# S5 heads of a two-layer hybrid backbone: rotation tables doubled on VectorE, swapped halves made by matmuls and multiplied out of PSUM

## The chip, the cores and the metric

One core of one Trainium2 chip. The metric is the device time of one execution in microseconds (us). TensorE is PE, VectorE DVE, ScalarE ACT, GpSimd POOL, SyncE SP; SP issues the DMAs spoken of here.

## The reference

Two layers over 128 context and 512 latent tokens, d_model 1024, fp32. Layer 0 has S5 heads and neighbourhood attention behind one input projection, layer 1 a gated DeltaNet; each has an MLP. The change lies in the S5 heads of layer 0:

```python
def _s5_scan(u, lam_re, lam_im, log_dt, b_re, b_im, c_re, c_im, x0):
    lam = lax.complex(lam_re, lam_im)
    lam_bar = jnp.exp(lam * jnp.exp(log_dt)[:, None])
    b_bar = ((lam_bar - 1) / lam)[..., None] * lax.complex(b_re, b_im)
    bu = jnp.einsum('gnp,blgp->blgn', b_bar, u)
    bu = bu.at[:, 0].add(lam_bar * x0)
    # x_t = lam_bar * x_(t-1) + bu_t
    _, xs = lax.associative_scan(comb, (a, bu), axis=1)
    y = jnp.einsum('gpn,blgn->blgp', c_mat, xs).real
    return y, xs[:, -1]
```

There are 32 groups of 16 channels with 64 complex states each, run forward and backward; the outputs of both directions and d * u are added, then gelu and a sigmoid gate. The context's last states are an output.

## The kernel before, in words

The tokens are cut into chunks of 8, 64 of latents and 16 of context, with one place more for each run's starting state: 82 columns, in segments of 65 and 17. The recurrence goes over chunks. The heads are worked in four **batches** of 8 groups (`s5_batch`), each with two **units**, one for each direction d (`s5_unit`). The real parts of the states lie on rows 0 to 63, the imaginary ones on rows 64 to 127.

A unit builds input weights `bp` on DVE (L783, L784; the sum L785 on POOL for d = 0), transposes them on PE (L790) and copies them out with ACT (L791). It builds output weights `ct` on DVE (L796 to L798), and multiplies the inputs `U` by the input weights on PE (L807). ACT copies the result to `W` (L809). The recurrence has a complex factor. The kernel turns the frame by e^(i theta e), so that the scan has a real factor: a rotation before (`rotate(W, SU, Z)`), the scan (L842, L844), a rotation back (`rotate(Y, AD, Sv)`). A rotation needs the other half of the rows: `swap` moves halves by two DMAs (L823, L824), DVE multiplies by the cosine (L830) and the sine (L831), in two segments of 65 and 17 chunks, and L832 adds, on POOL for d = 0.

`s5_tables` makes the cosine and sine tables of a batch: three doublings by `turns` on POOL (L861 to L866) from the first eight powers `s5e`, which `s5_params` makes with the same helper; then three DMAs of `rt` (L878, L879) bring both directions on all rows. `s5_taps` makes the taps of the convolution inside a chunk: small matmuls (L912), two ACT copies, DVE (L917, L919), then through DRAM into `L`. `s5_back` makes a batch's outputs with three matmuls to a group (L945, L947, L949) and its gelu (L962 to L967).

`even_s5` writes the four batches first, at a high priority, and then `project()` at a low one: the projection of queries, keys and values, 12 blocks of weights, each in two halves of 320 columns of 24 matmuls (L205 to L207; weights split in two parts, L194 on ACT and L196). ACT copies a half from the PSUM tile `pg` to `qs` (L1093, in the pool's buffers `us`); keys and values are transposed (L1096, L1108) into the PSUM tile `pc`. A scheduler sorts the whole into one order on each engine by readiness and priority. Buffers of a tag are handed out in the order of the program text, and an operation can't stand ahead of one that still holds its buffer. PSUM has four tags, `pa`, `pb`, `pc` and `pg`, with two buffers each; `us` has two, `rt` two, `bp`, `bpt` and the scratch `s5tmp` one. `proj_u`, the projection of the S5 inputs, runs before all of that; attention (L1001) after it.

```python
    def ps(self, tag):
        return self.psum.tile([128, 512], F32, name=tag, tag=tag, bufs=2)
...
            with tc.high_priority(offset=4000):
                cur = self.s5_batch(b, P, Us[b]) if b < 4 else None
...
        with tc.high_priority(offset=-500):
            project()
```

Of the kernel before, what the change touches and what calls it, by code (L numbers as in the profile page):

```python
# [20 lines left out]
T = 640          # 128 context tokens, then 512 latent tokens  # L21
HB = 320         # columns of one moving block
# [4 lines left out]
# columns of a half that belong to the context (0) and to the latents (1)  # L27
# [3 lines left out]
# ---------------------------------------------------------------- host: layout only  # L31
# [15 lines left out]
def layout(i):  # L47
    i = {k: np.asarray(v) for k, v in i.items()}
    f = np.float32
    o = {}  # L50
# [33 lines left out]
    for d in range(2):  # L84
# [14 lines left out]
    def bm(a):  # [2,32,64,16] -> [64, (d g), 16]  # L99
        return a.reshape(64, 64, 16).transpose(1, 0, 2)  # L100
# [5 lines left out]
         np.concatenate([cr, ci], 0), np.concatenate([ci, cr], 0)], 1))  # [128, 4, 64, 16]  # L106
    # d on the rows 32 i + p of (batch, round): group 8 b + 4 r + i
# [5 lines left out]
    # neighbourhood bias: [pair of heads, query, block kind, head, key]  # L113
# [15 lines left out]
    # constants of the shapes alone  # L129
    cst = np.zeros((128, 128 + 128 + 128 + 16 + 4 + 128), f)  # L130
# [8 lines left out]
    cst[:, 404:532] = np.kron(np.eye(4), np.tril(np.ones((32, 32))))  # L139
    o["cst"] = cst  # L140
# [7 lines left out]
# ---------------------------------------------------------------- the kernel  # L148
class Build:
# [93 lines left out]
    # -------- modulation  # L243
# [27 lines left out]
    def mod_half(self, l, nb, kh, P, tag="pc", row=None, dst=None):  # L271
        """Half of the contraction of 256 columns of the modulation."""
# [29 lines left out]
    def mod_scale(self, l, chunk, ni, name):  # L302
        """g * (1 + scale): [128, 8, 2]"""
# [7 lines left out]
    # -------- norms  # L311
# [14 lines left out]
    def rstd_bcast(self, st, tag="pc"):  # L326
        """rows of 1/rms over the columns of a half, in PSUM [128, 320]"""
# [13 lines left out]
    def norm_step(self, h, k, x, bc, a, sh, dst, first=False):  # L341
        """block k of a half; a, sh: [128, 2] scale and shift"""
# [15 lines left out]
    def norm_steps(self, h, x, st, a, sh, dst):  # L358
        """dst: list of 8 (hi, lo) tiles; a, sh: [128, 8, 2] scale and shift"""
# [6 lines left out]
    def start(self, x, dst, P):  # L366
        """the first norm and the start of the input projection, behind the modulation block by block"""
# [48 lines left out]
    def residual(self, x, l, chunk, m, h, p, st):  # L416
        """x[m] += gate * p, and the squares of the sum"""
# [51 lines left out]
    def seven(self, srcs, hn, Ts, evac, pool, after):  # L469
        """pairs of output tiles from the quarters"""  # L470
# [18 lines left out]
        def prep(i, j):  # L489
            """the left factor of a product, split"""  # L490
# [121 lines left out]
    # -------- S5: parameters  # L612
    def s5_params(self, P, sm, ring):
# [28 lines left out]
        def rnd(a, s1, s2=0.0):  # L642
            """round(a * s1 + s2)"""
# [27 lines left out]
        # sine and cosine of phi  # L671
# [26 lines left out]
        # (lam_bar - 1) / lam  # L698
# [23 lines left out]
        # powers of lam_bar: columns k for the forward pairs, 8 - k for the backward ones  # L722
# [25 lines left out]
        # e^{i theta}, theta = 8 phi, and the decay of eight steps  # L748
# [16 lines left out]
        self.turns(e[:, 0], e[:, 1], 1, 8, wk[:, 2], wk[:, 3], nc.gpsimd)  # L765

    def s5_unit(self, b, d, P, U, tb):
        """Batch b (8 groups), direction d: states of the chunks [128, 8, 82] and output weights."""
# [7 lines left out]
        # input weights, state by (s, p')  # L776
# [9 lines left out]
        bpt = self.tl([128, 8, 128], "bpt")  # L786
        for r in range(2):
# [3 lines left out]
            nc.scalar.activation(bpt[:, 4 * r:4 * r + 4].rearrange("p a b -> p (a b)"), pp, AF.Copy)  # L791
        # output weights, state by (k, p)
# [6 lines left out]
        # chunk inputs  # L799
        W = self.tl([128, 8, 82], "s5g")  # L800
        e0 = 1 - d
        for r in range(2):
            pw = self.ps("pb")
            for i in range(4):
                g = 4 * r + i
                n = 128 if g < 7 else 82
                nc.tensor.matmul(pw[:, 128 * i:128 * i + n], bpt[:, g], U[:, g * 82:g * 82 + n],  # L807
                                 start=True, stop=True)
            nc.scalar.activation(W[:, 4 * r:4 * r + 4, e0:e0 + 81],  # L809
                                 pw.rearrange("p (a b) -> p a b", a=4)[:, :, :81], AF.Copy)  # L810
        ex, ez = (0, 65) if d == 0 else (64, 81)
        V.tensor_copy(W[:, :, ex:ex + 1], self.s5x0[:, ps].unsqueeze(2))
        V.memset(W[:, :, ez:ez + 1], 0.0)
        # the recurrence, in the frame that turns with the state
        def segs(t):
            so = t[:, :, 0:65], t[:, :, 65:82]
            return so
        def tab(t):
            return (t, t[:, :, 0:17]) if d == 0 else (t[:, :, ::-1], t[:, :, 16::-1])
        sgn = self.cst[:, 400:401]  # L820
        def swap(src, name):
            o = self.tl([128, 8, 82], "s5g")
            nc.sync.dma_start(out=o[0:64], in_=src[64:128])  # L823
            nc.sync.dma_start(out=o[64:128], in_=src[0:64])  # L824
            return o
        def rotate(src, op, out):
            sw = swap(src, "sw")
            m = self.tl([128, 8, 82], "s5g")
            for so, c_, s_, w_, m_ in zip(segs(src), tab(tb[:, 0]), tab(tb[:, 1]), segs(sw), segs(m)):
                V.tensor_tensor(m_, so, c_, op=M)  # L830
                V.scalar_tensor_tensor(w_, w_, sgn, s_, op0=M, op1=M)  # L831
            (V if d else nc.gpsimd).tensor_tensor(out, m, sw, op=op)  # L832
        Z = self.tl([128, 8, 82], "s5g")
        rotate(W, SU, Z)
# [17 lines left out]
    def turns(self, c, s, n0, n1, w1, w2, eng):  # L852
        """doubles tables of e^{i theta e} from e = n0 on"""
        M, AD, SU = ALU.mult, ALU.add, ALU.subtract
        n = n0
        while n < n1:
            xr, xi = c[:, :, 1:n + 1], s[:, :, 1:n + 1]
            yr = c[:, :, n:n + 1].to_broadcast(list(xr.shape))
            yi = s[:, :, n:n + 1].to_broadcast(list(xr.shape))
            a1, a2 = w1[:, :, :n], w2[:, :, :n]  # L860
            eng.tensor_tensor(a1, xr, yr, op=M)  # L861
            eng.tensor_tensor(a2, xi, yi, op=M)
            eng.tensor_tensor(c[:, :, n + 1:2 * n + 1], a1, a2, op=SU)
            eng.tensor_tensor(a1, xr, yi, op=M)
            eng.tensor_tensor(a2, xi, yr, op=M)
            eng.tensor_tensor(s[:, :, n + 1:2 * n + 1], a1, a2, op=AD)  # L866
            n *= 2

    def s5_tables(self, b, P):
        """tables of e^{i theta e} of batch b: one direction on each half of the rows, then on both"""  # L870
        nc = self.nc
        t = [self.tl([128, 2, 8, 65], "rt") for d in range(2)]
        w1 = self.PA.tile([128, 8, 32], F32, name="rt1")
        w2 = self.PA.tile([128, 8, 32], F32, name="rt2")
        nc.gpsimd.tensor_copy(t[0][:, :, :, 0:9], self.s5e[:, :, 8 * b:8 * b + 8])
# [1118 lines left out]
```

## Time and profile before

| | us |
|---|---|
| median of 3 runs | 2053.17 |
| lowest and highest | 2051.83, 2055.7 |
| span of the profiled execution, first to last instruction | 2049.8 |
| median less that span (launch and end around it) | 3.4 |

For the profiled execution the profile gives the span alone, and no time of its own around it. In the profile a busy share says how much of a stretch an engine spent in instructions, the clock is the TensorE clock granted (1.00 is 2.4 GHz, 0.50 is 1.2 GHz), and a wait is put down to what was released last.

### The profile page before, as it was taken

The page shows a single profiled execution, that of the slowest core. Times are in us where ns is not written, and L with a number is a line of the kernel's source. Part 1 is how long each engine was busy: PE and PEld are TensorE (multiplying, and loading weights), DVE is VectorE, ACT ScalarE, POOL GpSimd, SP SyncE. Part 2 cuts the span into 40 slices and gives each one's busy share as a digit, 9 for nine tenths or more (in the row PEclk, how much of TensorE's full clock was granted, in tenths as well). Part 3 has the DMA queues.
Part 4 walks back from the last instruction along what each step waited for, and adds up shares of the span by engine and source line. Part 5 has one row for each costly group of instructions (what it writes and reads, how often), then busy time and mean ns, then how long its engine had stood idle before and what let it go on. Part 6 is the DMA issues. An engine that isn't in the chain of part 4 may idle for free. (4 is left out here: it accounts for less than half of the span.)

```text
span 2049.8 us, 35800 instructions
## 1 busy us (share of the span) xinstructions
PE 1818.7 (89%) x13476; PEld 1703.2 (83%) x13476; DVE 1371.1 (67%) x2791; ACT 830.1 (40%) x1804; POOL 1004.6 (49%) x821
## 2 busy tenths in 40 slices
PE   5778779999999999998877889798989799999988
PEld 3777757897898989998877888787788799998987
DVE  8877767459457382838679998774558828375563
ACT  4333336444224251535554555354225314243342
POOL 2866635453355454654355545522245526464561
PEclk9989889999999999999998999899989899999999
DMA  8335498524422222332476468768833122222221
GB/s 307 109 112 141 118 279 277 212 99 150 143 80 75 73 83 63 123 113 73 153 219 192 120 195 241 219 176 273 263 125 130 66 73 72 77 72 79 73 91 55
DMA packets 206984, 286.61 MB, mean 140 GB/s; under 512 B 54878, under 2 KB 138236, under 8 KB 206812
## 3 DMA queue, kind: packets, MB, share of 16 engines
q1 hardware_dynamic: 206812, 284.33, 44.2%
q8 instruction: 107, 1.75, 0.4%
q14 instruction: 65, 0.53, 0.1%
HBM read 228.87 MB, written 46.82 MB: 135 GB/s over the span
## 5 line engine op out<-in xcount | busy, mean ns | idle before, releaser
L196 POOL TENSOR_TENSOR wlo<-raw,whi 128x1024 fp32r<-128x1024 f32 (+1 forms) x145 | 341.5, 2357 | 392.1 <-ACT whi L194 384.3
L194 ACT ACTIVATE whi<-raw 128x1024 fp32r<-128x1024 f32 (+1 forms) x153 | 152.8, 999 | 287.5 <-PE pg L206 149.2
L205 PE MATMUL pg<-hidh,whi 128*128 128x320 f32 (+2 forms) x576 | 181.8, 316 | 9.1 <-DVE msq L550 4.6
L207 PE MATMUL pg<-hidh,wlo 128*128 128x320 f32 (+2 forms) x576 | 181.2, 315 | 7.4 <-POOL wlo L196 7.4
L206 PE MATMUL pg<-hidl,whi 128*128 128x320 f32 (+2 forms) x576 | 181.0, 314 | 2.2 <-DVE hidl L576 2.2
L205 PE MATMUL pg<-h10h,whi 128*128 128x320 f32 x472 | 157.6, 334 | 14.8 <-DVE cb L1718 6.4
L422 DVE SCALAR_TENSOR_TENSOR x<-pg,mod,x 128x128 f32<-128x128 f32 (+2 forms) x132 | 53.7, 436 | 172.0 <-PE pg L207 172.0
L207 PE MATMUL pg<-h10h,wlo 128*128 128x320 f32 x472 | 154.4, 327 | 1.2 <-POOL wlo L196 1.2
L206 PE MATMUL pg<-h10l,whi 128*128 128x320 f32 x472 | 154.5, 327 | 0.0
L507 POOL TENSOR_TENSOR wq<-S,wq 128x512 fp32r<-128x512 f32 x78 | 113.5, 1459 | 76.5 <-ACT wq L506 76.5
L205 PE MATMUL pa<-hidh,whi 128*128 128x320 f32 x448 | 138.0, 310 | 0.8 <-ACT whi L194 0.8
L206 PE MATMUL pa<-hidl,whi 128*128 128x320 f32 x448 | 138.3, 309 | 0.0
L207 PE MATMUL pa<-hidh,wlo 128*128 128x320 f32 x448 | 137.6, 309 | 0.0
L422 DVE SCALAR_TENSOR_TENSOR x<-pa,mod,x 128x128 f32<-128x128 f32 (+2 forms) x108 | 43.8, 435 | 130.6 <-PE pa L207 130.6
L205 PEld LDWEIGHTS pg<-hidh,whi 128*128 128x128 f32 x576 | 109.8, 191 | 12.4 <-DVE msq L550 5.3
L207 PEld LDWEIGHTS pg<-hidh,wlo 128*128 128x128 f32 x576 | 110.0, 191 | 9.2 <-POOL wlo L196 9.2
L206 PEld LDWEIGHTS pg<-hidl,whi 128*128 128x128 f32 x576 | 110.1, 191 | 3.3 <-DVE hidl L576 3.3
L205 PEld LDWEIGHTS pg<-h10h,whi 128*128 128x128 f32 x472 | 95.0, 201 | 18.7 <-DVE cb L1718 7.5
L507 POOL TENSOR_TENSOR wq<-raw,wq 128x512 fp32r<-128x512 f32 x56 | 77.0, 1385 | 68.2 <-ACT wq L506 66.0
L1318 DVE SCALAR_TENSOR_TENSOR cv<-cb,cw,cv 128x642 f32<-128x642 f32 x90 | 94.5, 1051 | 10.8 <-ACT cv L1315 9.9
L207 PEld LDWEIGHTS pg<-h10h,wlo 128*128 128x128 f32 x472 | 94.5, 200 | 1.6 <-POOL wlo L196 1.4
L206 PEld LDWEIGHTS pg<-h10l,whi 128*128 128x128 f32 x472 | 94.8, 201 | 0.6 <-issue 0.4
(743 smaller groups left out, 6032.1 us busy)
## 6 DMA issues: line engine op xcount, KB each, us to landing
raw<-in_wff SPq DMA_DIRECT2D x104, 512.0 KB
mraw<-in_wmod SPq DMA_DIRECT2D x96, 512.0 KB
raw<-in_wino SPq DMA_DIRECT2D x33, 512.0 KB
rawx<-in_wff SPq DMA_DIRECT2D x24, 512.0 KB
raw<-in_wine SPq DMA_DIRECT2D x16, 512.0 KB
cka<-pd SPq DMA_DIRECT2D x28, 256.0 KB
ckb<-pd SPq DMA_DIRECT2D x28, 256.0 KB
s5g<-s5g SPq DMA_DIRECT2D x32, 164.0 KB
```

What stands on the lines that cost most here:

```text
L194: nc.scalar.activation(hi[:, :kt], raw[:, :kt], AF.Copy)
L196: (nc.vector if self.lov and self.nw % self.lov else nc.gpsimd).tensor_tensor(lo[:, :kt], raw[:, :kt], hi[:, :kt], op=ALU.subtract)
L205: nc.tensor.matmul(p[:, :n], hi[:, k], xh[:, s], start=(k == 0), stop=False)
L206: nc.tensor.matmul(p[:, :n], hi[:, k], xl[:, s], start=False, stop=False)
L207: nc.tensor.matmul(p[:, :n], lo[:, k], xh[:, s], start=False, stop=(k == kt - 1))
L422: nc.vector.scalar_tensor_tensor(x[m][:, s], p[:, ls], g, x[m][:, s], op0=ALU.mult, op1=ALU.add)
L507: nc.gpsimd.tensor_tensor(t[:, 4:8], src, t[:, 0:4], op=SU)
L1318: V.scalar_tensor_tensor(cv, cb[m][:, t:t + 642], cw[:, t:t + 1], cv, op0=M, op1=AD)
```

## The change

- `turns` takes both tables as one tile and runs on DVE: for each doubling two products over cosine and sine together, then one subtraction and one addition over half of it. Both its callers are on DVE now; the scratch is `s5tmp`.
- The tables are 82 chunks wide, so a rotation no longer has segments. ACT copies one direction's rows (L874), two DMAs bring the others (L875, L876 of the new kernel), and ACT negates the sine of the upper rows (L878) and repeats the columns (L879, L880).
- The input weights carry their first 64 columns twice (`bpt` 128 x 8 x 192, one more ACT copy). Eight more matmuls a unit give the inputs with halves swapped, in `pa`. The evictions to `W` and the swap's DMAs go. DVE multiplies both PSUM tiles by the tables, one of them in place, and subtracts (L818 to L820), in two halves of 324 columns.
- For the rotation back, PE multiplies `Y` by a permutation `halves` (L841, two matmuls of 328 columns into `pc`), and DVE multiplies in place in PSUM and adds (L844, L845). All additions of rotations are on DVE.
- `s5g` has five buffers, before six.

```diff
 def s5_unit
-        bpt = self.tl([128, 8, 128], "bpt")
+        bpt = self.tl([128, 8, 192], "bpt")
...
-            nc.scalar.activation(bpt[:, 4 * r:4 * r + 4].rearrange("p a b -> p (a b)"), pp, AF.Copy)
+            nc.scalar.activation(bpt[:, 4 * r:4 * r + 4, 0:128], pp, AF.Copy)
+            nc.scalar.activation(bpt[:, 4 * r:4 * r + 4, 128:192], pp[:, :, 0:64], AF.Copy)
...
-        rotate(W, SU, Z)
+            pw, pv = self.ps("pb"), self.ps("pa")
+            for p, c0 in ((pw, 0), (pv, 64)):
+                for i in range(4):
+                    g = 4 * r + i
+                    n = 128 if g < 7 else 82
+                    nc.tensor.matmul(p[:, 128 * i:128 * i + n], bpt[:, g, c0:c0 + 128], U[:, g * 82:g * 82 + n],
+                                     start=True, stop=True)
+            pw, pv = (p.rearrange("p (a b) -> p a b", a=4)[:, :, :81] for p in (pw, pv))
+            rs, es = slice(4 * r, 4 * r + 4), slice(e0, e0 + 81)
+            V.tensor_tensor(Z[:, rs, es], pw, tc_[:, rs, es], op=M)
+            V.tensor_tensor(pv, pv, ts_[:, rs, es], op=M)
+            V.tensor_tensor(Z[:, rs, es], Z[:, rs, es], pv, op=SU)
...
-        rotate(Y, AD, Sv)
+        m = Z
+        V.tensor_tensor(m, Y, tc_, op=M)
+        for r in range(2):
+            p = self.ps("pc")[:, :328]
+            nc.tensor.matmul(p, self.halves, fl(Y)[:, 328 * r:328 * r + 328], start=True, stop=True)
+            p = p.rearrange("p (a b) -> p a b", a=4)
+            rs = slice(4 * r, 4 * r + 4)
+            V.tensor_tensor(p, p, ts_[:, rs], op=M)
+            V.tensor_tensor(Sv[:, rs], m[:, rs], p, op=AD)
...
 def turns
+        while n < n1:
+            x, y = t[:, :, :, 1:n + 1], t[:, :, :, n + 1:2 * n + 1]
...
+            V.tensor_tensor(a, x, yi, op=M)
+            V.tensor_tensor(y, x, yr, op=M)
+            V.tensor_tensor(y[:, 0], y[:, 0], a[:, 1], op=SU)
+            V.tensor_tensor(y[:, 1], y[:, 1], a[:, 0], op=AD)
...
 def s5_tables
-        self.turns(t[0][:, 0], t[0][:, 1], 8, 64, w1, w2, nc.gpsimd)
-        for r in range(2):
-            nc.sync.dma_start(out=t[1][64 * r:64 * r + 64], in_=t[0][64:128])
-        nc.sync.dma_start(out=t[0][64:128], in_=t[0][0:64])
+        self.turns(t[0][:, :, :, 0:65], 8, 64, w)
+        nc.scalar.activation(t[1][64:128, :, :, 17:82], t[0][64:128, :, :, 0:65], AF.Copy)
+        nc.sync.dma_start(out=t[1][0:64, :, :, 17:82], in_=t[1][64:128, :, :, 17:82])
+        nc.sync.dma_start(out=t[0][64:128, :, :, 0:65], in_=t[0][0:64, :, :, 0:65])
+        for d in range(2):
+            nc.scalar.activation(t[d][0:64, 1, :, 17 * d:17 * d + 65], t[d][0:64, 1, :, 17 * d:17 * d + 65], AF.Copy, scale=-1.0)
```

How the change moves instructions on PE. Before, in the first S5 batch (d = 1): matmuls of the fourth projection block (`pg_2277`, `pg_2305`), transposes of the third (L1108) and the S5 inputs (L807) stand among each other.

```order
L205 MATMUL pg_2277<-h00h7_126,whi_2272 128x320
L1108 MATMUL pc_2256<-cst_69,qs_2226 128x128 x3
L1108 MATMUL pc_2262<-cst_69,qs_2226 128x128
L807 MATMUL pb_1193<-s5s_1060,bpt_1174 128x128 x4
L807 MATMUL pb_1199<-s5s_1060,bpt_1174 128x128 x3
L807 MATMUL pb_1199<-s5s_1060,bpt_1174 128x82
L1108 MATMUL pc_2262<-cst_69,qs_2226 128x128 x3
L206 MATMUL pg_2277<-h00l7_127,whi_2272 128x320
L207 MATMUL pg_2277<-h00h7_126,wlo_2273 128x320
L205 MATMUL pg_2305<-h00h0_112,whi_2272 128x320
```

All of the S5 work before stands like this, a few rows at a time between projection steps.

After, the same place, the last half of the first batch's inputs and what follows (L814 the inputs, L841 the rotation back, L913 the taps, L792 the next batch's transposes):

```order
L814 MATMUL pb_1206<-s5s_1056,bpt_1172 128x82
L814 MATMUL pa_1194<-s5s_1056,bpt_1172 128x128 x4
L814 MATMUL pa_1207<-s5s_1056,bpt_1172 128x128 x3
L814 MATMUL pa_1207<-s5s_1056,bpt_1172 128x82
L841 MATMUL pc_1158<-s5g_1154,halves_1047 128x328
L841 MATMUL pc_1162<-s5g_1154,halves_1047 128x328
L913 MATMUL pb_1239<-ct_1117,Bb1_923 32x128 x8
L913 MATMUL pb_1248<-ct_1187,Bb1_923 32x128 x8
L841 MATMUL pc_1229<-s5g_1225,halves_1047 128x328
L841 MATMUL pc_1233<-s5g_1225,halves_1047 128x328
L792 MATMUL pb_1311<-cst_69,bp_1305 128x128 x4
```

No projection step stands here; the first four blocks are ahead of it, and rows of S5 alone follow for all four batches, some 170. This is their end, with the last batch's L841 and outputs (`pb_2040`, `pb_2054`):

```order
L946 MATMUL pb_1995<-s5s_1622,ct_1583 128x81
L948 MATMUL pb_1995<-s5s_1693,ct_1653 128x81
L950 MATMUL pb_1995<-s5s_1273,L_1780 128x81
L841 MATMUL pc_1944<-s5g_1940,halves_1047 128x328
L841 MATMUL pc_1948<-s5g_1940,halves_1047 128x328
L946 MATMUL pb_2040<-s5s_1871,ct_1832 128x128
L946 MATMUL pb_2054<-s5s_1871,ct_1832 128x128
L1097 MATMUL pc_2154<-cst_69,qs_2125 128x128
L948 MATMUL pb_2040<-s5s_1942,ct_1902 128x128
```

The first transpose of the projection, L1097 of its first block, stands only behind the last L841. The first step of the fifth block (`pg_2372`) comes twelve rows further on; before, the fifth block's first step (`pg_2344`) stood between the first batch's taps and the second batch's transposes.

On ACT after, between the taps of the first batch and the second batch's weights, with `rt_1282` and `rt_1283` the second batch's tables:

```order
L916 ACTIVATE kk_1238<-pb_1239 128x2x128
L917 ACTIVATE kk_1238<-pb_1248 128x2x112
L874 ACTIVATE rt_1283<-rt_1282 64x16x65
L878 ACTIVATE rt_1283<-rt_1283 64x8x65
L794 ACTIVATE bpt_1310<-pb_1311 128x4x128
L795 ACTIVATE bpt_1310<-pb_1311 128x4x64
L880 ACTIVATE rt_1283<-rt_1283 128x16x17
L794 ACTIVATE bpt_1310<-pb_1318 128x4x128
L795 ACTIVATE bpt_1310<-pb_1318 128x4x64
```

The negation of the sine (L878), which needs the table's DMA, stands ahead of the copies of the input weights out of PSUM (L794). Before, nothing of the tables was on ACT.

## Rows read from the trace of the kernel before

**Rows 1.** The page: span, and TensorE's busy time, share and instructions.
```profile
span 2049.8 us, 35800 instructions
PE 1818.7 (89%) x13476; PEld 1703.2 (83%) x13476; DVE 1371.1 (67%) x2791; ACT 830.1 (40%) x1804; POOL 1004.6 (49%) x821
```

**Rows 2.** Windows: us, then busy us (instructions) of PE, PEld, DVE, ACT, POOL; clock, DMA share, GB/s.
```profile
80.00:254.00 174.00, 137.68 (x996) 133.66 (x996) 132.14 (x163) 56.90 (x112) 118.71 (x104) 0.88 0.45 122
268.00:376.00 108.00, 106.65 (x875) 82.80 (x876) 79.97 (x199) 62.95 (x181) 54.69 (x51) 0.97 0.82 265
125.00:150.00 25.00, 17.72 (x127) 16.95 (x128) 22.41 (x32) 9.31 (x19) 17.60 (x15) 0.74 0.36 109
```

**Rows 3.** Timeline of PE: start us, duration us, line, tiles, shapes, count, idle before.
```profile
80.40 0.64 PE L205 MATMUL pg<-h00h,whi 128*128 128x320 f32 x1 [7.03 <-ACT us L1061]
80.83 0.47 PE L206 MATMUL pg<-h00l,whi 128*128 128x320 f32 x1
81.10 0.47 PE L207 MATMUL pg<-h00h,wlo 128*128 128x320 f32 x1
...
110.32 1.04 PE L790 MATMUL pb<-cst,bp 128*128 128x128 f32 x8
...
114.57 1.91 PE L807 MATMUL pb<-s5s,bpt 128*128 128x128 f32 x16
...
118.27 0.31 PE L205 MATMUL pg<-h00h,whi 128*128 128x320 f32 x1
118.42 0.30 PE L206 MATMUL pg<-h00l,whi 128*128 128x320 f32 x1
...
127.96 1.93 PE L912 MATMUL pb<-ct,Bb 128*32 128x128 f32 x32 [8.36 <-ACT s5g L809]
...
252.72 0.93 PE L1108 MATMUL pc<-cst,qs 128*128 128x128 f32 x7
268.29 0.77 PE L1001 MATMUL pa<-kT,qz 128*128 128x128 f32 x2 [14.64 <-DMA qz<-qkv]
...
274.78 1.08 PE L912 MATMUL pb<-ct,Bb 128*32 128x128 f32 x32
```

**Rows 4.** PE's waits from 75 to 290 us: total us, times, longest.
```profile
PE pb L912 <- ACT s5g L809: 21.7, 3, 8.4
...
PE pb L790 <- DVE kk L917: 4.3, 1, 4.3
PE pb L945 <- DVE kk L917: 4.3, 1, 4.3
PE pb L790 <- POOL bp L785: 2.5, 1, 2.5
```

**Rows 5.** DVE from 75 to 290 us by line and shape: busy us, mean ns, idle.
```profile
L830 DVE TENSOR_TENSOR s5g<-s5g,rt 128x520 f32<-128x520 f32 x16 | 13.6, 853 | 28.6 <-DMA rt<-rt 28.4
...
L844 DVE TENSOR_TENSOR_SCAN s5g<-s5g 128x656 f32<-128x656 f32 x4 | 6.6, 1650 | 0.1
...
L830 DVE TENSOR_TENSOR s5g<-s5g,rt 128x136 f32<-128x136 f32 x16 | 4.7, 292 | 0.0
...
L849 DVE COPY s5fin<-s5s 128x8 f32<-128x8 f32 x7 | 2.5, 352 | 0.0
...
L919 DVE SCALAR_TENSOR_TENSOR kk<-cst,s5d,kk 128x16 f32<-128x16 f32 x8 | 1.9, 271 | 0.0
```

**Rows 6.** Timeline of DVE, three places.
```profile
85.35 1.22 DVE L783 TENSOR_TENSOR bp<-pwr,Bb 128x1024 f32<-128x1024 f32 x1 [2.82 <-POOL s5e L866]
...
121.89 0.91 DVE L830 TENSOR_TENSOR s5g<-s5g,rt 128x520 f32<-128x520 f32 x2 [11.96 <-DMA rt<-rt]
...
124.80 1.22 DVE L783 TENSOR_TENSOR bp<-pwr,Bb 128x1024 f32<-128x1024 f32 x1
```

**Rows 7.** POOL from 75 to 290 us by line and shape.
```profile
L785 POOL TENSOR_TENSOR bp<-bp,s5tmp 128x1024 f32<-128x1024 f32 x4 | 10.8, 2696 | 2.5 <-DVE s5tmp L784 1.2 <-DVE s5g L838 1.2
...
L863 POOL TENSOR_TENSOR rt<-rt,rt 128x256 f32<-128x256 f32 x4 | 6.8, 1698 | 0.3
```

**Rows 8.** ACT from 75 to 290 us by line and shape.
```profile
L791 ACT ACTIVATE bpt<-pb 128x512 f32<-128x512 f32 x16 | 9.3, 602 | 14.7 <-PE pb L790 9.8 <-issue 4.9
...
L809 ACT ACTIVATE s5g<-pb 128x324 f32<-128x324 f32 x16 | 6.6, 441 | 46.4 <-POOL s5g L832 34.6 <-PE pb L807 10.1 <-POOL rt L866 1.6
```

More of the change, by code (lines that the diff above doesn't have):

```diff
@@ L128, in layout @@
     o["cv"] = np.ascontiguousarray(i["cache_na_v"][0, 0].reshape(128, 512))
-    cst = np.zeros((128, 128 + 128 + 128 + 16 + 4 + 128), f)
+    cst = np.zeros((128, 128 + 128 + 128 + 16 + 4 + 128 + 128), f)
     cst[:, :128] = np.eye(128)
@@ L139, in layout @@
     cst[:, 404:532] = np.kron(np.eye(4), np.tril(np.ones((32, 32))))
+    cst[:, 532:660] = np.roll(np.eye(128), 64, 0)
     o["cst"] = cst
@@ L764, in s5_params @@
                 nc.gpsimd.tensor_copy(e[64 * d:64 * d + 64, n, :, 1:2], a[64 * d:64 * d + 64, 32 * d:32 * d + 32].unsqueeze(2))
-        self.turns(e[:, 0], e[:, 1], 1, 8, wk[:, 2], wk[:, 3], nc.gpsimd)
+        self.turns(e, 1, 8, wk.rearrange("p a b c -> p (a b c)"))
     def s5_unit(self, b, d, P, U, tb):
@@ L790, in s5_unit @@
                 nc.tensor.transpose(pp[:, 128 * i:128 * i + 128], bp[:, 4 * r + i], self.ident)
-            nc.scalar.activation(bpt[:, 4 * r:4 * r + 4].rearrange("p a b -> p (a b)"), pp, AF.Copy)
+            pp = pp.rearrange("p (a b) -> p a b", a=4)
+            nc.scalar.activation(bpt[:, 4 * r:4 * r + 4, 0:128], pp, AF.Copy)
+            nc.scalar.activation(bpt[:, 4 * r:4 * r + 4, 128:192], pp[:, :, 0:64], AF.Copy)
         sh = [128, 8, 9, 16]
@@ L798, in s5_unit @@
         V.tensor_tensor(ct, ct, t2, op=SU)
-        W = self.tl([128, 8, 82], "s5g")
         e0 = 1 - d
+        ex, ez = (0, 65) if d == 0 else (64, 81)
+        tc_, ts_ = (tb[:, n] if d == 0 else tb[:, n, :, ::-1] for n in range(2))
+        Z = self.tl([128, 8, 82], "s5g")
         for r in range(2):
[L803 to L833, printed above, removed]
-        rotate(W, SU, Z)
+            pw, pv = self.ps("pb"), self.ps("pa")
@@ L835, in s5_unit @@
+            V.tensor_tensor(pv, pv, ts_[:, rs, es], op=M)
+            V.tensor_tensor(Z[:, rs, es], Z[:, rs, es], pv, op=SU)
+        V.tensor_copy(Z[:, :, ex:ex + 1], self.s5x0[:, ps].unsqueeze(2))
+        if d:
+            V.memset(Z[:, :, ez:ez + 1], 0.0)
         d0 = self.tl([128, 8, 82], "s5g")
@@ L850, in s5_unit, with turns @@
         return ct, S
-    def turns(self, c, s, n0, n1, w1, w2, eng):
+    def turns(self, t, n0, n1, w):
+        V = self.nc.vector
         M, AD, SU = ALU.mult, ALU.add, ALU.subtract
-        n = n0
+        n, g = n0, t.shape[2]
         while n < n1:
[L857 to L866, printed above, removed]
+            x, y = t[:, :, :, 1:n + 1], t[:, :, :, n + 1:2 * n + 1]
+            sh = [128, 2, g, n]
+            yr, yi = (t[:, k, :, n:n + 1].unsqueeze(1).to_broadcast(sh) for k in range(2))
+            a = w[:, :2 * g * n].rearrange("p (k g e) -> p k g e", k=2, g=g)
+            V.tensor_tensor(a, x, yi, op=M)
+            V.tensor_tensor(y, x, yr, op=M)
+            V.tensor_tensor(y[:, 0], y[:, 0], a[:, 1], op=SU)
+            V.tensor_tensor(y[:, 1], y[:, 1], a[:, 0], op=AD)
             n *= 2
@@ L871, in s5_tables @@
         nc = self.nc
[L872 to L875, printed above, removed]
-        self.turns(t[0][:, 0], t[0][:, 1], 8, 64, w1, w2, nc.gpsimd)
-        for r in range(2):
-            nc.sync.dma_start(out=t[1][64 * r:64 * r + 64], in_=t[0][64:128])
-        nc.sync.dma_start(out=t[0][64:128], in_=t[0][0:64])
+        t = [self.tl([128, 2, 8, 82], "rt") for d in range(2)]
+        w = self.tl([128, 8, 9, 16], "s5tmp").rearrange("p a b c -> p (a b c)")
+        nc.vector.tensor_copy(t[0][:, :, :, 0:9], self.s5e[:, :, 8 * b:8 * b + 8])
+        self.turns(t[0][:, :, :, 0:65], 8, 64, w)
[4 more added lines that the diff above has]
+            nc.scalar.activation(t[d][0:64, 1, :, 17 * d:17 * d + 65], t[d][0:64, 1, :, 17 * d:17 * d + 65], AF.Copy, scale=-1.0)
+        nc.scalar.activation(t[0][:, :, :, 65:82], t[0][:, :, :, 0:17], AF.Copy)
+        nc.scalar.activation(t[1][:, :, :, 0:17], t[1][:, :, :, 17:34], AF.Copy)
         return t
@@ L1843, in last @@
                     nc.sync.dma_start(out=dst[:, cs], in_=o)
-    BUFS = dict(s5g=6, s5s=6, s5o=3, bp=1, bpt=1, ct=4, rt=2, vts=2,
+    BUFS = dict(s5g=5, s5s=6, s5o=3, bp=1, bpt=1, ct=4, rt=2, vts=2,
                 cv=3, khT=2, ktok=2, vtok=2, cb=2, otok=2, osq=1)
@@ L1859, in run @@
             self.cst = self.cp.tile([128, 532], F32, name="cst")
-            nc.sync.dma_start(out=self.cst, in_=A["cst"])
+            nc.sync.dma_start(out=self.cst, in_=A["cst"][:, 0:532])
             self.ident = self.cst[:, 0:128]
@@ L1900, in run @@
                     self.P = P
+                    self.halves = P.tile([128, 128], F32, name="halves")
+                    nc.sync.dma_start(out=self.halves, in_=A["cst"][:, 532:660])
                     self.mraw = "", 0, [(self.wp, "raw", 2), (self.wp, "whi", 2), (self.wp, "wlo", 2), (P, "vts", 2)][2:]
```

## The prediction

> **What bounds the kernel now.** I read the page first. TensorE (PE) is busy for 89% of a 2049.8 us span [rows 1], so a stage is slow where PE stands still or does more. The change touches one stage only, the input projection of layer 0 with the S5 heads, so I read its windows next. From 80 to 254 us PE is busy 137.68 of 174 us at a mean granted clock of 0.88; from 268 to 376 us, attention and gate, PE is busy 106.65 of 108 [rows 2]. The reader should see two different regimes: in the first PE waits now and then and often runs at the lower clock (0.74 from 125 to 150 us), the second is PE alone.
>
> The timeline shows what fills the first. A projection step is three matmuls of 320 columns that start 0.147 us apart at the full clock (118.27, 118.42) and 0.27 apart at the lower one (80.83, 81.10) [rows 3]. A block of two times 24 is 7.06 us, and there are twelve; S5 work lies between them. At the end PE finishes the projection at 253.65 us and waits 14.64 us for attention's loads [rows 3]. The list of PE's waits then shows what S5 costs there: 21.7 us in three waits of the taps (L912), two of 4.3 behind VectorE, one of 2.5 behind GpSimd [rows 4], together 32.8 us. These are what the change aims at; S5 is otherwise hidden under projection steps.
>
> **The order is the largest term.** L841, the second rotation's swap, takes PSUM buffers named "pc", of which there are two, and it takes sixteen of them. The projection's transposes use the same two, and the program text has all S5 batches ahead of the projection. So the first transpose (pc_2154) has to come behind the last L841, and with it what hangs on it: the copies out of the projection's PSUM ("pg", two buffers) into "us" (two buffers). The order of the changed kernel shows exactly this: four projection blocks, then about 170 rows of S5 alone, then the other eight. PE still waits in S5, and has nothing to put there.
>
> **The length of the S5 stretch.** VectorE (DVE) carries its chain. I price its operations by a line through the 136-element rotation, 0.292 us [rows 5], and a clean 1024-element product, 1.22 us at 124.80 [rows 6]: 0.15 us + 1.045 ns an element. (The 520-element one, 0.853, lies above the line, with GpSimd working beside it, and gives the upper end.) Per batch:
> - input and output weights, unchanged: 5 products of 1024 at 1.22 and 6 of 1152 at 1.35 = 14.2 us;
> - each unit: six operations of 324 from PSUM and four of 328 at 0.49 = 4.9, one of 656 at 0.84, the scan 1.65, two small copies 0.35 each [rows 5] = 8.1, and two units 16.2. No row reads PSUM with two inputs at this size; the ends are 0.49 and 0.57 (by a line through the 520 row), and I take the lower, since GpSimd falls nearly idle;
> - tables, new on DVE: three doublings with two full-size products and two halves. At 128, 256, 512 elements, with halves of 64, 128, 256, that is 1.0 + 1.4 + 2.2, and a copy 0.3 = 4.9. The GpSimd table it replaces ends what DVE waits for at 121.89 (11.96 us) [rows 6];
> - taps 0.7 [rows 5], three operations of 656 behind a batch 2.5.
> Sum 38.5 us a batch, 154 for four, on an engine whose queue runs in order.
>
> PE's own additions are small beside this. Sixteen matmul records (two to a matmul) in 1.91 us [rows 3] is 0.12 a record. Per unit there are 16 more records and two 328-column swaps, which I price by their columns as five records each: 3 us, 25 for eight units. GpSimd loses its tables (1.70 for a 256-column step) and the rotations' additions but keeps four additions of 2.70 us [rows 7]; that relief is worth nothing where DVE is the chain. ScalarE loses the W evictions (0.441 each) and gains smaller copies of the kind that take 0.60 for 512 [rows 8].
>
> The end of the stretch: projection starts at 80.40 as before; four blocks are 28.2 us, and some 3 more for the lower clock at their start: PE comes to S5 at 111.6. By then DVE has tables, the first weights and half of the output products of batch 0 behind it, since these wait for no PE. What is left of batch 0 is 16.2 of rotations and 7.8 of weights, and a first PE burst of 2: 26 us. Three batches follow at 38.5 plus waits that nothing covers: transposes 1.04 (eight records), eviction 0.60, inputs 1.9 times two, the swap behind each scan, and the table's DMAs that stand ahead of the weight evictions in ScalarE's queue. Their sum is nearly 10 a batch; half of it lies under other DVE work, so I take 5. PE is done some 5 before DVE's last operations: 111.6 + 26 + 3 x 43.5 - 5 = 263.
>
> **Then the rest.** Eight blocks 56.5, 36 transposes 4, the last batch's outputs 5.5 (48 records at 0.12), 5 for clock and buffers until steps run close: 71. The projection then ends at 334 instead of 253.65, 80 later. Back comes what the last batch did on PE inside attention before: taps 1.08 at 274.78 [rows 3] and its 48 records, 6.5. Attention's own loads and wait I leave as they are. Net +74. The profiled execution's span is 2049.8, 3.4 under the median 2053.17: 2049.8 + 74 + 3.4 = **2127**. Break-even is an S5 stretch that ends on PE at 189, that is 19 us a batch, half of DVE's own load.
>
> Edits at nothing: the eight powers (s5e) move to DVE, about 3 us, against the 2.82 DVE waited for them at 85.35 [rows 6]; the constant's extra load lies beside others; five instead of six "s5g" buffers, since the swapped tiles are gone. DeltaNet's rows far behind are also shuffled somewhat by the same scheduler; no row prices this, I allow 8 either way, about the largest single wait in [rows 4].
>
> **Rivals.**
> *DVE is never kept waiting.* The 5 us are covered: the stretch ends at 248, +59, and 10 less if attention's wait of 14.64 shrinks because its neighbours' transfers have long landed. 2102 to 2112. For it: DVE runs its products between rotations. Against: one "bp", one "bpt", one scratch buffer tie it to PE and GpSimd.
> *The clock stays low.* PE in the stretch works in bursts. This trace shows it granted the lower level after such waits: the 32 tap records took 1.93 us after 8.36 idle, and 1.08 at 274.78 [rows 3]. If all S5 bursts run so, the uncovered part grows by about 8 a batch, and the late start of the blocks by 3: +101, 2154. The Trainium skill, page "TensorE: Matmul & The Clock Gate", section "HAM oscillation — how this bites in real kernels", states that matmul bursts separated by waits begin cold each time; by that rule this is the outcome, and the 1.93 against 1.08 agrees with it. I give it less than the first forecast because most of PE's time would lie under DVE's chain anyway.
> *Other side: faster.* If projection steps did fill S5's waits, PE's 32.8 us of waits would go and 25 of new matmuls come: 8 less, and 2 to 5 more from a clock that no longer falls: 2040 to 2045. It decides if the stretch takes under 19 us a batch. Against it stands the order itself, which is fixed in the program, and 38.5 us of DVE operations.
> *The change doesn't do what it says*: the swap DMAs do go and DVE no longer waits for them, but that only matters if the stage is as before.
>
> **Chances.** Forecast case (2112 to 2145) 0.55; DVE never waits (2092 to 2112) 0.18; low clock (2145 to 2162) 0.17; faster 0.05; no difference 0.02; still slower, with queues blocking each other, 0.03. The range 2092 to 2162 holds the first three. A measurement here tells 0.2% (4 us) from none. Slower 0.93, same 0.02, faster 0.05.
>
> **What would show it.** In the profile after: no L206 to L208 of the projection between about 112 and 263 us, PE mostly idle there at a lower clock, DVE nearly full; then eight blocks back to back with DVE and ScalarE light; attention from about 348. PE's largest waits will name DVE's rotations in place of L809. Wrong if projection steps run among L814 and L841, if DVE is well under 80% in the stretch (then a DMA or ScalarE's queue decides), or if the stretch takes under 30 us a batch.

## The result and the profile after

The changed kernel takes 2086.09 us (median of four, 2080.97 to 2087.28) against 2053.4 of the kernel before on the same chip: a ratio of 1.0154, interval 1.0142 to 1.0166. It is slower by 33 us, where 74 had been forecast, and 6 us under the range. Direction and mechanism hold; the size is half.

The page after, answering to [rows 1]:

```profile
span 2085.3 us, 36052 instructions
...
PE 1845.5 (89%) x13636; PEld 1724.4 (83%) x13636; DVE 1371.3 (66%) x2867; ACT 841.5 (40%) x1824; POOL 897.6 (43%) x719
```

PE's busy time grew by 26.8 us (25 were forecast), the span by 35.5. The windows of the S5-alone stretch and of what follows (columns as in [rows 2]):

```profile
112.00:239.00 127.00, 82.02 (x633) 71.64 (x632) 113.04 (x225) 35.86 (x74) 7.24 (x5) 0.80 0.24 61
239.00:308.00 69.00, 64.74 (x453) 63.99 (x451) 13.94 (x15) 29.06 (x53) 7.66 (x7) 0.99 0.55 174
```

In 127 us PE is busy 82.02, at a clock of 0.80, and DVE 113.04, or 89%. "Mostly idle", as the forecast had PE there, it is not: 65% of the stretch is busy. Behind it PE is nearly full, 64.74 of 69 us. The timeline of PE shows the steps. L792 at 108.72, 140.16, 174.05 and 210.71 opens the four batches, L841 at 234.78 is the last swap, L1097 the first transpose of the projection, L208 its last step, L1002 the start of attention:

```profile
108.72 1.04 PE L792 MATMUL pb<-cst,bp 128*128 128x128 f32 x8
...
140.16 1.97 PE L792 MATMUL pb<-cst,bp 128*128 128x128 f32 x8 [6.80 <-POOL bp L786]
...
174.05 1.97 PE L792 MATMUL pb<-cst,bp 128*128 128x128 f32 x8 [9.83 <-POOL bp L786]
...
210.71 1.97 PE L792 MATMUL pb<-cst,bp 128*128 128x128 f32 x8 [10.59 <-POOL bp L786]
...
234.78 1.31 PE L841 MATMUL pc<-s5g,halves 128*128 128x328 f32 x4
...
237.17 0.30 PE L1097 MATMUL pc<-cst,qs 128*128 128x128 f32 x1 [0.64 <-DVE s5s L845]
...
301.69 0.31 PE L208 MATMUL pg<-h00h,wlo 128*128 128x320 f32 x1
...
305.97 1.63 PE L1109 MATMUL pc<-cst,qs 128*128 128x128 f32 x7 [3.86 <-ACT qs L1094]
...
308.81 0.77 PE L1002 MATMUL pa<-kT,qz 128*128 128x128 f32 x2 [1.21 <-DMA qz<-qkv]
```

No projection step lies between 108 and 237 us apart from those of the first four blocks. So the stretch is the forecast one, but it ends at 237 and not at 263. The eight blocks take until 302, transposes until 307.6: 70 us, 71 forecast. And attention begins at once: its wait is 1.21 us, before 14.64 [rows 3]. PE's waits from 75 to 340 us no longer name L809 [rows 4]. The largest, 27.2 us in three waits at the openings of the batches, names the sum of the input weights on GpSimd, L786, which itself follows two products of DVE; DVE's scans (L831, L833) come behind with 8.0. The forecast had DVE's rotations as the largest:

```profile
PE pb L792 <- POOL bp L786: 27.2, 3, 10.6
...
PE pc L841 <- DVE s5g L833: 4.9, 1, 4.9
...
PE pc L841 <- DVE s5g L831: 3.1, 3, 1.6
```

To compare stages over kernels I use one mark: the first residual of layer 0, behind attention and gate. The row of that line gives durations in ns (least, median, greatest), then the starts of its first and last instruction in us; the mark is the first of these (the kernel before, then the changed one):

```profile
L422 DVE SCALAR_TENSOR_TENSOR x<-pg,mod,x x132: 335/408/553, 390.7 to 1920.3; 128x128 f32<-128x128 f32 x44, 128x192 f32<-128x192 f32 x44, 128x320 f32<-128x320 f32 x44
```

```profile
L423 DVE SCALAR_TENSOR_TENSOR x<-pg,mod,x x132: 331/408/552, 421.2 to 1957.7; 128x128 f32<-128x128 f32 x44, 128x192 f32<-128x192 f32 x44, 128x320 f32<-128x320 f32 x44
```

The mark is 30.5 us later, 421.2 against 390.7. From there to the end of the span it is 1664.1 us, before 1659.1: another 5.

### The profile page after: what moved, and what is told of

The parts are those of the page before. It is cut to its first block, busy times and chain, and to the rows that moved or that the text cites. A ratio compares the mean times of both kernels' runs of the same rounds, so it can differ in the third digit from the quotient of the medians.

```text
span 2085.3 us, 36052 instructions
## 1 busy us (share of the span) xinstructions
PE 1845.5 (89%) x13636; PEld 1724.4 (83%) x13636; DVE 1371.3 (66%) x2867; ACT 841.5 (40%) x1824; POOL 897.6 (43%) x719
## 4 chain that ended last, share of the span: by engine, by line
PE 18%; DVE 18%; DMA 6%; issue 5%; POOL 3%; ACT 2%; SPq 1%; POOLq 0%; DVEq 0%; ACTq 0%
PE pg L206 3%; DVE cv L1319 3%; PE pg L208 3%; PE pg L207 3%; DVE sbt L1422 2%; DVE ub L1424 2%; POOL wq L508 2%; PE pa L208 2%; PE pa L206 2%; PE pa L207 2%; DMA cgq<-gbd 1%; DVE hidl L577 1%; DVE msq L575 1%; DMA ed<-gbg 1%; DMA gD<-or 1%
## 5 line engine op out<-in xcount | busy, mean ns | idle before, releaser
L197 POOL TENSOR_TENSOR wlo<-raw,whi 128x1024 fp32r<-128x1024 f32 (+1 forms) x145 | 336.0, 2320 | 422.6 <-ACT whi L195 411.5
L208 PE MATMUL pg<-hidh,wlo 128*128 128x320 f32 (+2 forms) x576 | 181.9, 316 | 8.6 <-POOL wlo L197 8.6
L208 PE MATMUL pg<-h10h,wlo 128*128 128x320 f32 x472 | 156.0, 331 | 0.0
L208 PE MATMUL pa<-hidh,wlo 128*128 128x320 f32 x448 | 137.6, 309 | 0.0
L208 PEld LDWEIGHTS pg<-hidh,wlo 128*128 128x128 f32 x576 | 110.5, 192 | 10.4 <-POOL wlo L197 10.4
L208 PEld LDWEIGHTS pg<-h10h,wlo 128*128 128x128 f32 x472 | 95.8, 203 | 0.4
```

The source lines that it names most:

```text
L197: (nc.vector if self.lov and self.nw % self.lov else nc.gpsimd).tensor_tensor(lo[:, :kt], raw[:, :kt], hi[:, :kt], op=ALU.subtract)
```

## The experiments

All medians beside the kernel before on the same chip; its own medians in these comparisons lie between 2053.31 and 2054.98, so that kernels from two of them compare to some 2 us at best. The stage is the mark above, the rest is the span less that mark; both come from one profiled execution of each kernel, up to 5 us from its median.

| kernel | median, us | ratio [interval] | stage | rest |
|---|---|---|---|---|
| before | 2053.31 to 2054.98 | 1 | 390.7 | 1659.1 |
| changed | 2086.09 | 1.0154 [1.0142, 1.0166] | 421.2 | 1664.1 |
| swap_pa | 2031.95 | 0.9884 [0.9852, 0.9916] | 365.1 | 1660.2 |
| pc_in_before | 2112.39 | 1.0284 [1.0243, 1.0324] | 447.0 | 1659.3 |
| bp_on_dve | 2078.48 | 1.0108 [1.0070, 1.0145] | 417.0 | 1661.0 |
| swap_pa_bp | 2027.38 | 0.9862 [0.9828, 0.9896] | 360.6 | 1668.5 |
| tab_only | 2037.6 | 0.9914 [0.9893, 0.9935] | 377.4 | 1662.1 |
| swap_pa_tabpool | 2018.32 | 0.9820 [0.9796, 0.9845] | 365.8 | 1651.1 |
| swap_dma_back | 2047.95 | 0.9971 [0.9956, 0.9986] | 356.9 | 1685.3 |
| swap_dma_bp | 2015.26 | 0.9813 [0.9790, 0.9837] | 352.9 | 1659.7 |
| swap_dma_tab_bp | 2032.0 | 0.9887 [0.9864, 0.9909] | 367.7 | 1666.4 |

**One word: other buffers for the swap (swap_pa).**

```diff
-            p = self.ps("pc")[:, :328]
+            p = self.ps("pa")[:, :328]
```

> The changed kernel with one edit: the PSUM tile of the rotation back (L841) takes its buffers from pa and not from pc. The order on PE then has S5 rows among projection steps again. Theory 1 (the order costs the time: sixteen pc buffers ahead of the projection's transposes hold the projection back): the S5-alone stretch of 127 us goes, PE waits little, and the time falls by 30 us or more, to 2035 to 2056 us. Rival (the added work costs the time: 160 more matmul records, tables on VectorE, operands read from PSUM): it stays at 2075 to 2090 us.

Theory 1 holds: 2031.95, 54 us under the changed kernel, 3 under the range that the theory gave, and 1.2% faster than the kernel before. All the added work is still there. In the first stage PE is now busy 163.64 of 174 us at a clock of 0.96 (before 137.68 at 0.88, [rows 2]):

```profile
80.00:254.00 174.00, 163.64 (x1264) 155.81 (x1264) 152.84 (x270) 70.46 (x137) 24.31 (x12) 0.96 0.47 134
```

Its waits for S5 are down to a few; the loads of attention are waited for 5.9 us, before 14.6:

```profile
PE pc L1002 <- DMA qz<-qkv: 5.9, 2, 4.5
PE pb L792 <- DVE s5g L818: 3.4, 3, 2.0
```

**The order alone (pc_in_before).**

```diff
+        for r in range(2):
+            p = self.ps("pc")[:, :4]
+            nc.tensor.matmul(p, self.ident, fl(Y)[:, 328 * r:328 * r + 4], start=True, stop=True)
         S = self.tl([128, 656], "s5s")
```

> The kernel before with one addition: behind each scan two matmuls of 4 columns into pc tiles that nobody reads, where the changed kernel has L841. Everything else, tables on GpSimd and swaps by DMA too, is as before. The order on PE becomes four projection blocks, S5 alone, then the other blocks. Theory 1: the time rises although the work is the same, and by more than in the changed kernel, since here table and swap DMAs stand in the S5 chain: 2100 to 2140 us. Rival (the changed kernel is slow by its added work): 2050 to 2060 us, as before.

2112.39: 2.8% slower by sixteen tiny matmuls (L847) that nobody reads. PE is busy 55.68 of the same 127 us, at a clock of 0.66, and waits for the scans:

```profile
112.00:239.00 127.00, 55.68 (x391) 50.69 (x390) 98.79 (x135) 21.77 (x42) 80.51 (x68) 0.66 0.38 96
```

```profile
PE pc L847 <- DVE s5g L842: 52.1, 4, 18.5
```

The stage is 56 us later than before. So the order alone makes a loss, and a larger one than the changed kernel's; in the clumped order the change is worth 26 us at the mark (447.0 against 421.2). That it is the tag, and not matmuls behind each scan as such, swap_pa shows: there L841 stands behind each scan too, in pa.

**VectorE's queue as the chain (bp_on_dve).**

```diff
-        (V if d else nc.gpsimd).tensor_tensor(bpv, bpv, t1[:, :, :8], op=AD)
+        V.tensor_tensor(bpv, bpv, t1[:, :, :8], op=AD)
```

> The changed kernel with one edit: the sum of the input weights for d = 0 (L786) runs on VectorE too, no longer on GpSimd. Theory (in the S5-alone stretch VectorE's queue is the chain, and every wait and slowed product in it lengthens the stretch): per batch the wait of 2.5 us and what the slowed product beside GpSimd loses go, and 1.2 come, for three or four batches 4 to 10 us less: 2076 to 2082 us. Rival (PE's bursts at the lower clock and their latencies set the length): within 3 us of the changed kernel, 2083 to 2089 us.

2078.48, 7.6 us less by the medians, 4.2 at the mark. The timeline of PE shows where: the batches open at 139.37, 171.58 and 206.25 instead of 140.16, 174.05 and 210.71, and the first transpose comes 3.1 us sooner:

```profile
139.37 1.94 PE L792 MATMUL pb<-cst,bp 128*128 128x128 f32 x8 [5.65 <-DVE bp L786]
...
171.58 1.94 PE L792 MATMUL pb<-cst,bp 128*128 128x128 f32 x8 [8.68 <-DVE bp L786]
...
206.25 1.94 PE L792 MATMUL pb<-cst,bp 128*128 128x128 f32 x8 [9.19 <-DVE bp L786]
...
234.05 0.30 PE L1097 MATMUL pc<-cst,qs 128*128 128x128 f32 x1 [0.64 <-DVE s5s L845]
```

Two batches are about 2 us shorter each, as the theory has it; the last one, from its opening to the transpose, is 1.3 longer. The median's other 3 us lie behind the mark, where the two traces differ by 3.1. With 3.1 at the transpose and 4.2 at the mark this stands at the edge of the rival's 3 us, and the intervals of the two ratios touch: the run leans to the theory and doesn't settle it. DVE's own waits, below, weigh more.

**Both edits (swap_pa_bp).**

> Both edits together: rotation back in pa, and L786 on VectorE. Theory 1: with the projection running under S5 the VectorE chain has slack, so the second edit is worth little: within 5 us of the version with the first edit alone, 2035 to 2056 us. Rival (VectorE sets the pace in the interleaved order too): 4 to 10 us below the version with the first edit alone.

2027.38, 4.6 less than swap_pa, 4.5 at the mark: at the edge of what theory 1 allowed (its range for the total missed, as with swap_pa) and inside the rival's interval, so this pair doesn't tell them apart.

**Tables alone on VectorE (tab_only).** In the kernel before:

```diff
-        nc.gpsimd.tensor_copy(t[0][:, :, :, 0:9], self.s5e[:, :, 8 * b:8 * b + 8])
-        self.turns(t[0][:, 0], t[0][:, 1], 8, 64, w1, w2, nc.gpsimd)
+        nc.vector.tensor_copy(t[0][:, :, :, 0:9], self.s5e[:, :, 8 * b:8 * b + 8])
+        self.turns(t[0][:, 0], t[0][:, 1], 8, 64, w1, w2, nc.vector)
```

> The kernel before with the tables of a batch doubled on VectorE (the six-operation form, three DMAs as before); rotations, swaps by DMA and their sums on GpSimd stay. Theory A (the late table is what held S5 and with it PE's waits of 21.7 us): the 28.4 us that VectorE waits for the table's DMA fall to under 10, VectorE takes on some 22 us, and the time falls by 5 to 20 us. Rival (the swaps by DMA and the sums on GpSimd hold it): within 4 us of the kernel before.

2037.6, 16 us faster than before, 13 of them at the mark. DVE's wait for the table's DMA falls from 28.4 us, the idle time of L830 in [rows 5], to 11.5:

```profile
DVE s5g L830 <- DMA rt<-rt: 11.5, 4, 3.8
```

Theory A holds, though not to under 10. But the order moved too: attention begins at 219.5, against 268.29 before, and the last batch runs wholly inside it. So the 13 us are not shown to be the table's wait alone.

**Tables back on GpSimd, with the swap in pa (swap_pa_tabpool).**

```diff
-        nc.vector.tensor_copy(t[0][:, :, :, 0:9], self.s5e[:, :, 8 * b:8 * b + 8])
-        self.turns(t[0][:, :, :, 0:65], 8, 64, w)
+        nc.gpsimd.tensor_copy(t[0][:, :, :, 0:9], self.s5e[:, :, 8 * b:8 * b + 8])
+        self.turns(t[0][:, :, :, 0:65], 8, 64, w, nc.gpsimd)
```

> The version with the rotation back in pa, but the tables of a batch doubled on GpSimd (the four-operation form, scratch from the s5g buffers). Theory A (tables on VectorE are part of the gain): VectorE waits for the table again, the time rises by 5 to 15 us over the version it comes from, 2037 to 2047 us. Rival (with the projection running under S5 a late table is covered): within 4 us of 2032.

2018.32: faster by 14 us, which neither expected. The stage is the same (365.8 against 365.1); what differs lies in the rest, 1651.1 against 1660.2 in the traces, 9.1 apart, and stays unexplained; the medians of four runs each, on two chips, lie further apart than that. At the stage the rival holds.

**The swap back by DMA (swap_dma_back).** From swap_pa:

```diff
+        sw = self.tl([128, 8, 82], "s5g")
+        nc.sync.dma_start(out=sw[0:64], in_=Y[64:128])
+        nc.sync.dma_start(out=sw[64:128], in_=Y[0:64])
         V.tensor_tensor(m, Y, tc_, op=M)
...
+        V.tensor_tensor(sw, sw, ts_, op=M)
+        V.tensor_tensor(Sv, m, sw, op=AD)
```

> The version with the rotation back in pa, but its swap made by two DMAs again instead of L841; VectorE multiplies out of SBUF. It takes 32 matmul records (11.9 us of PE in the changed kernel) away and puts 16 DMAs into SP's queue. Theory B (in the interleaved order PE is the bound, so a swap on PE costs its own time): 4 to 10 us faster than the version it comes from, 2022 to 2028 us. Rival (the DMA's latency stands in VectorE's chain and attention's loads queue behind the swaps): 3 to 10 us slower, 2035 to 2042 us.

By the total the rival has the direction, and not the size: 2047.95, 16 us slower than swap_pa, 6 over its range. By the mark theory B wins:

```profile
L423 DVE SCALAR_TENSOR_TENSOR x<-pg,mod,x x132: 334/408/553, 356.9 to 1914.7; 128x128 f32<-128x128 f32 x44, 128x192 f32<-128x192 f32 x44, 128x320 f32<-128x320 f32 x44
```

The stage is 8.2 us shorter, and the rest 25 us longer. The rest is the same program, but not in the same order: a scheduler sorts it, and a changed first layer changes some hundred places in the order of layer 1's DeltaNet on PE. In pc_in_before and swap_pa_bp that order is the one of the kernel before, row by row; their rest is 1659.3 and 1668.5 in one execution each (the second one 3.5 above its median), so under 10 us of a difference in the rest can be scatter. The next variant has the DMA swap and nearly the old order behind.

**The same with the old order in DeltaNet (swap_dma_bp).** L786 on VectorE, as in bp_on_dve, on top of swap_dma_back:

> The version with the rotation back's swap by DMA, and L786 on VectorE. With this edit the order of PE's rows in layer 1's DeltaNet falls back to that of the kernel before, but for eight places; in the version it comes from that order was another, and its time from the first residual to the end was 1685 us where the kernel before took 1659. Theory C (the loss of the DMA version was the order in DeltaNet, not the swap): first residual at 352 to 357 us, 1655 to 1665 us from there, 2012 to 2026 us in all. Rival (DMA swaps themselves cost, here or later): 2038 us or more.

2015.26, 33 us faster than swap_dma_back and, with swap_pa_tabpool (2018.32, the intervals overlap), the fastest. The stage moved by 4, the rest by 26, to 1659.7:

```profile
L423 DVE SCALAR_TENSOR_TENSOR x<-pg,mod,x x132: 338/408/553, 352.9 to 1885.0; 128x128 f32<-128x128 f32 x44, 128x192 f32<-128x192 f32 x44, 128x320 f32<-128x320 f32 x44
```

Theory C holds. The rows say where the 26 us went: from the first convolution of the DeltaNet (L1317) to the start of the last L208 of its output projection swap_dma_back takes 626.4 us and this kernel 598.1; the other nine kernels take 588.8 to 603.8.

```profile
L1317 DVE SCALAR_TENSOR_TENSOR cv<-cb,cw,cv x90: 758/878/3097, 920.8 to 1240.7; 128x642 f32<-128x642 f32 x90
L208 PE MATMUL pg<-ozh,wlo x96: 304/309/633, 1454.5 to 1547.2; 128*128 128x320 f32 x96
```

```profile
L1317 DVE SCALAR_TENSOR_TENSOR cv<-cb,cw,cv x90: 760/879/3101, 919.8 to 1257.8; 128x642 f32<-128x642 f32 x90
L208 PE MATMUL pg<-ozh,wlo x96: 304/309/468, 1397.8 to 1517.9; 128*128 128x320 f32 x96
```

Not every changed order costs: the changed kernel and swap_pa have some hundred places changed there too and take 602.0 and 598.1. What in the order of swap_dma_back makes it slow is not known.

The swap back on PE costs 7.7 us of stage in the interleaved order (360.6 with it, 352.9 without, L786 on VectorE in both), as a stage in which PE is the bound would have it: PE is busy 166.07 of 174. (Attention also begins sooner, at 232.3 against 248.9, so part of it may be the order.)

```profile
80.00:254.00 174.00, 166.07 (x1310) 156.94 (x1310) 157.75 (x283) 78.32 (x164) 15.88 (x14) 0.97 0.61 168
```

**Tables on GpSimd once more (swap_dma_tab_bp).**

> The same with the tables of a batch on GpSimd; PE's order in DeltaNet again near that of the kernel before (six places differ). Theory (in the interleaved order PE is the bound and tables on GpSimd are covered): first residual within 4 us of the version without this edit, and the total within 5 us of it. Rival (tables on GpSimd save VectorE time that counts): 6 us or more faster.

Both fall: 2032.0, 17 slower, 14.8 of it at the mark (367.7). DVE waits 12.3 us for an ACT copy of the tables (L877, which is L879 of the changed kernel):

```profile
DVE s5g L818 <- ACT rt L877: 12.3, 4, 5.5
```

So tables on VectorE are worth 15 us of stage here, and nothing measurable beside the swap in pa. In swap_pa_tabpool DVE waits 6.6 us for the same copy. Why the late table costs nothing there and 15 us here stays open.

## Why the prediction was right in kind and wrong in size

**Right: the order is the largest term.** It was read from the buffers and the order, before any run. pc_in_before makes the loss with no other part of the change, and swap_pa takes it away with every other part in place. PE's additions (25 us against 26.8 of busy time), the restart (71 against 70), and the last batch's work that leaves attention were near.

**Wrong: "Sum 38.5 us a batch" and "I take 5" for waits.** The forecast had a batch every 43.5 us; the middle ones open 33.9 and 36.7 us apart, and the first transpose comes at 237 instead of 263, 26 us sooner. The single operations were priced well, as the rows of DVE from 75 to 340 us show (mean ns: 492 and 481 for the halves from PSUM against 0.49 us taken, 832 against 0.84; the scan 1513 against 1650):

```profile
L819 DVE TENSOR_TENSOR pa<-pa,rt 128x324 f32<-128x324 f32 x16 | 7.8, 492 | 0.6 <-PE pa L814 0.6
...
L818 DVE TENSOR_TENSOR s5g<-pb,rt 128x324 f32<-128x324 f32 x16 | 7.4, 481 | 1.3 <-PE pb L814 1.1 <-issue 0.2
L838 DVE TENSOR_TENSOR s5g<-s5g,rt 128x656 f32<-128x656 f32 x8 | 6.7, 832 | 0.0
L833 DVE TENSOR_TENSOR_SCAN s5g<-s5g 128x656 f32<-128x656 f32 x4 | 6.1, 1513 | 0.0
```

The durations were summed as if one began where the last ended, and they overlap: in this stretch of DVE's timeline a product of 1.22 us starts 1.13 before the next:

```profile
174.03 1.36 DVE L801 TENSOR_TENSOR s5tmp<-pwi,s5bc 128x1152 f32<-128x1152 f32 x1 [2.54 <-POOL bp L786]
...
176.70 1.22 DVE L784 TENSOR_TENSOR bp<-pwr,Bb 128x1024 f32<-128x1024 f32 x1
...
177.83 1.22 DVE L785 TENSOR_TENSOR s5tmp<-pwi,Bb 128x1024 f32<-128x1024 f32 x1
```

A batch has some 60 operations, most of them short ones. The windows from one opening to the next count overlap once:

```profile
140.16:174.05 33.89, 21.18 (x169) 18.68 (x169) 30.64 (x61) 9.05 (x19) 2.34 (x1) 0.80 0.24 53
174.05:210.71 36.66, 22.49 (x168) 20.12 (x168) 32.73 (x64) 10.57 (x21) 2.45 (x2) 0.78 0.28 75
```

DVE's load is 31 to 33 us a batch and not 38.5, and it stands still for 3.3 and 3.9 and not 5; three times the difference between 43.5 and their mean distance, 35.3, makes 25 of the 26 us. The durations of the second window's rows sum to 37.2, so overlap is worth 4.5 of the 5.8 and the two small copies and the scan the rest. The trace of before had it to see: the product in front of the one at 124.80 [rows 6] starts 1.14 us sooner and lasts 1.22:

```profile
123.66 1.22 DVE L784 TENSOR_TENSOR s5tmp<-pwi,Bb 128x1024 f32<-128x1024 f32 x1
```

The 2.54 for GpSimd's sum at 174.03 is the regular wait. For PE, the other candidate, DVE waits only 3.2 us of the 127:

```profile
DVE pc L844 <- PE pc L841: 1.5, 1, 1.5
...
DVE s5g L818 <- PE pb L814: 1.1, 1, 1.1
DVE pa L819 <- PE pa L814: 0.6, 1, 0.6
```

**Wrong: "Attention's own loads and wait I leave as they are".** That is 13.4 us more. SyncE's queue shows why the wait was there. Before, from the start of the projection's last step at 250.30 on, it still issued S5's transfers and a weight load, and the keys' load (kT) came at 264.19 (rows: start, duration, line, tiles, count):

```profile
253.35 1.15 SPq L878 DMA_DIRECT2D rt<-rt  x2
...
255.28 1.21 SPq L268 DMA_DIRECT2D mraw<-in_wmod  x1
...
258.99 1.15 SPq L823 DMA_DIRECT2D s5g<-s5g  x1
...
261.36 2.73 SPq L955 DMA_DIRECT2D s5o<-yd  x6
...
264.19 0.38 SPq L981 DMA_DIRECT2D kT<-qkv  x1
```

After, S5's last transfer through yd goes out by 286.3 and only loads of its results (s5o<-zd) are left, so the keys' load goes out 0.55 us behind the start of the last step at 301.69:

```profile
300.92 1.27 SPq L1160 DMA_DIRECT2D s5o<-zd  x3
...
302.24 0.42 SPq L982 DMA_DIRECT2D kT<-qkv  x1
```

The forecast named this as "10 less" in a rival and did not put it in the sum, though the change moves the whole of S5 ahead of these loads. That it is SP's queue is read from the rows; it was not tried by itself.

**The rest.** Attention and gate take 10 us less from first matmul to mark (122.4 before, 112.4 after), 6.5 forecast. DeltaNet's shuffle was allowed 8 either way; the whole rest is 5 longer in the changed kernel, which is inside the scatter. Together: 74 - 26 - 13.4 - 3.5 + 5 = 36, the span's 35.5.

**The rivals.** "DVE is never kept waiting" is nearest; with its wait for attention it gave 2102 at best, since it rested on the same 38.5. The low clock was half right. The first burst of each later batch ran at the lower clock (L792 1.97 us at 140.16, behind 6.80 of idle time, 1.04 at 108.72). The Trainium skill, page "TensorE: Matmul & The Clock Gate", section "HAM oscillation — how this bites in real kernels", says that bursts separated by waits begin cold; these bursts agree. Not each wait did it: the swap at 155.04, behind 1.64 us, ran at the upper level (1.37 us, against 1.31 at 234.78 with no wait).

```profile
155.04 1.37 PE L841 MATMUL pc<-s5g,halves 128*128 128x328 f32 x4 [1.64 <-DVE s5g L831]
```

The forecast's condition held for the bursts, and the time did not follow: DVE, which makes the chain, waited for PE for 3.2 us in all. "Other side: faster" rested on projection steps filling S5's waits; with pa buffers they do, and it forecast 2040 to 2045 where swap_pa gives 2032. The mechanism was right and the order of the changed kernel shut it out.

## What to carry to other kernels

Where a scheduler hands out buffers in program order, a tag is a queue: ask of each new user of a tag what comes behind it in the text, and choose the tag by that. Sum an engine's load by the distance between starts, not by recorded durations. And compare variants at a mark behind the changed stage as well as by the total: here an unchanged stage far behind moved by 26 us with its order, and by the total alone a better stage looked worse.

## What the runs showed of the hardware

VectorE products with an operand in PSUM, one of them in place, took 0.48 to 0.50 us for 324 columns, the 0.49 that the forecast's line through products out of SBUF gives. A product of 1152 took 3.55 us beside an operation of GpSimd that began 0.07 sooner and took 2.41, where the next one took 1.36: as if it ran only behind the other (that one ends at 108.42, this one 1.21 us later). The two rows of DVE, then the one of GpSimd:

```profile
106.08 3.55 DVE L801 TENSOR_TENSOR s5tmp<-pwi,s5bc 128x1152 f32<-128x1152 f32 x1 [2.52 <-POOL bp L786]
109.66 1.36 DVE L802 TENSOR_TENSOR ct<-ct,s5tmp 128x1152 f32<-128x1152 f32 x1
```

```profile
106.01 2.41 POOL L197 TENSOR_TENSOR wlo<-raw,whi 128x1024 fp32r<-128x1024 f32 x1
```

The Trainium skill, page "SBUF — State Buffer", section "SBUF: two separate sides", says that VectorE and GpSimd share a pair of ports, which the first to start holds for its whole instruction, and counts among the cases a VectorE operation with two inputs in SBUF beside a GpSimd operation that reads SBUF. Both hold for these two, and the rows agree. It cost this kernel little, since GpSimd is busy for 7.24 of the 127 us of the stretch.
